# One-column sums of a modulation vector: four blocks in one slot and one bank, or a block a slot and a bank each

## The chip, the cores and the metric

The kernel runs on one core of a Trainium2 chip. The metric is the device time of one execution in microseconds (us), as the median of several runs. TensorE (PE) does the matrix products, VectorE (DVE) and ScalarE (ACT) the work on vectors, GpSimd (POOL) some subtractions, and SyncE (SP) issues most of the transfers. PE's results land in PSUM, which has eight banks; DVE and ACT take them out of there.

## The reference, cut to what matters

An encoder layer is applied to two requests (256 and 1024 rows of 1024 columns). A conditioning vector `c` of each request sets shifts, scales and gates:

```
mod = einsum('bd,de->be', silu(c), ada_w) + ada_b       # e has 6 * 1024 columns
sh1, sc1, gt1, sh2, sc2, gt2 = split(mod, 6)
h = rmsnorm(x, norm1_g) * (1 + sc1) + sh1
z = h @ w_in                                            # latents, q/k/v of two attentions, two gates
...
x = x + gt1 * (merged @ w_out)
h2 = rmsnorm(x, norm2_g) * (1 + sc2) + sh2
...                                                     # feed-forward with gt2
```

`sh1` and `sc1` are needed at once. The other four (gt1, sh2, sc2, gt2) are needed only behind both attentions: this is "the later modulation". `mod` has one value for each column and request.

## The kernel before, in words

Everything runs once through, as a list of stages written out by hand. Products are in float32 split into a rounded high part and a low rest (three products for one), so PE is the busiest engine. The framework that places the instructions on the engines follows the order of the Python text, but lets an instruction that it thinks ready go ahead of one that it thinks is not; buffers of one tag are handed round.

The stage of this change is the windowed (dilated) attention, lines 841 to 961. Its outer loop takes six steps (three head groups by two pairs, line 855), its inner loop ten row blocks `i` (line 935). In a row block PE computes scores (L890, into the banks S0 and S1), DVE adds the bias and finds the extreme (L895), ACT takes the exponential (L900), PE transposes (L910), DVE or ACT copies out (L914, L916), and PE multiplies by the values (L925), which DVE or ACT copies out (L931, L929).

Between these steps the loop draws on generators, that is, on Python functions that issue a few instructions and then `yield`:

- `side` (`filler`, line 672) issues the products of the gates from `block` (line 656; L99). A chunk of 512 or 256 columns takes one bank of the tag "pp" through 24 matmuls, in four draws, and is then copied out by ACT (L665) or DVE (L663). It is drawn 19 times in ten row blocks.
- `side2` (`norms`, line 695) is drawn once in each row block; six of its draws make sums of the same form in "pp" (L711), and one a transpose.
- `more` loads the queries and keys of the next step (L628, and a subtraction by DVE).
- `side3` (`modulation`, line 759) is the one that the change touches. It is drawn three times in two row blocks: 15 draws a step, 90 in all six.

`modulation` goes over eight chunks `c` of 512 columns of `mod`. For each it loads eight blocks of `ada_w` (L765, 256 KB each, tag "ad") and adds each, times the value of `c`, to an accumulator `acc` of 128 x 512 for either request (tag "mo", one buffer; DVE, L768 for the first block, L770 for the others). After each of the eight blocks it yields. What is left is the sum over the 128 partitions of `acc`: a matmul with 128 columns of `acc` as the weights and one column of ones gives 128 sums in one column. Four blocks of 128 columns by two requests make eight matmuls (L775), all into one bank of "pp"; as float32 each is two instructions on PE, so 16 a chunk. Two additions by DVE (line 777, shown at the helper's line L77 as `t<-pp,t`) take the bank's eight columns, add `ada_b` and write `modT`. Then it yields once more: nine draws a chunk, 72 in all.

The tag "pp" has two buffers (lines 354 and 355), shared by `block`, `norms`, `modulation`, the transposed statistics at each step's end (L953, copied by L955) and `gate_rows` (L189). After the six steps what is left of `side` is run out, then `gain_cols` (L184, which reads `modT`) and `gate_rows` (L189, which reads it too) follow.

Of the kernel before, what the change touches and what calls it, by code (L numbers as in the profile page):

```python
# [12 lines left out]
ALU = mybir.AluOpType  # L13
# [3 lines left out]
P = 128  # L17
# [28 lines left out]
def kernel(  # L46
# [8 lines left out]
    nc = tc.nc  # L55
    count = [0]

    def mk(pool, shape, dt=F32, tag=None, bufs=None):
        count[0] += 1
        kw = {}  # L60
        if bufs is not None:
            kw["bufs"] = bufs
        return pool.tile(shape, dt, name=f"{tag or 't'}_{count[0]}", tag=tag or f"u{count[0]}", **kw)
# [12 lines left out]
    def dve_tt(out, a, b, op):  # L76
        nc.vector.tensor_tensor(out=out, in0=a, in1=b, op=op)  # L77
# [30 lines left out]
    ones = mk(const, [P, P])  # L108
    nc.vector.memset(ones, 1.0)
    vecT = mk(const, [P, V_END])  # L110
    modT = mk(const, [P, 6 * KD, 2])
# [106 lines left out]
    def X():  # L218
        return mk(psX[1], [P, 2, 512], tag="X", bufs=4)
# [107 lines left out]
    abT = mk(hcm[1], [P, 6 * KD])  # L327
# [15 lines left out]
    def bank(tag, bufs=1):  # L343
        return mk(psC[1], [P, 512], tag=tag, bufs=bufs)
# [9 lines left out]
    def pp():  # L354
        return bank("pp", 2)
# [397 lines left out]
    def ad_tile(dt=F32):  # L753
        return mk(cpl, [P, 512], dt, tag="ad", bufs=AD)
# [4 lines left out]
    def modulation():  # L759

        for c in range(4, 12):
            acc = mk(cpl, [P, 2, 512], tag="mo", bufs=1)
            for k in range(KD):
                w = ad_tile()
                nc.sync.dma_start(out=w, in_=ada_w[k * P:(k + 1) * P, 512 * c:512 * c + 512])  # L765
                for r in range(2):
                    if k == 0:
                        nc.vector.tensor_scalar(out=acc[:, r], in0=w, scalar1=cT[:, k, r:r + 1], scalar2=None, op0=ALU.mult)  # L768
                    else:
                        nc.vector.scalar_tensor_tensor(out=acc[:, r], in0=w, scalar=cT[:, k, r:r + 1], in1=acc[:, r], op0=ALU.mult, op1=ALU.add)  # L770
                yield
            ps = pp()[:, 0:8]
            for b in range(4):
                for r in range(2):
                    nc.tensor.matmul(ps[:, 2 * b + r:2 * b + r + 1], lhsT=acc[:, r, P * b:P * b + P], rhs=ones[:, 0:1], start=True, stop=True)  # L775
            for r in range(2):
                dve_tt(modT[:, 4 * c:4 * c + 4, r], ps.rearrange("p (b r) -> p b r", r=2)[:, :, r], abT[:, 4 * c:4 * c + 4], ALU.add)
            yield

    SIDE = 19  # L780

# [66 lines left out]
    rest, LD, SPEED = [], 1, 2  # L848

    side, side2, side3 = filler(), norms(), modulation()  # L850
    values(0)
    run(queries_keys(0, 0, qk[0, 0]))
    for _ in range(8):
        next(side)
    for pair, g in steps:
# [96 lines left out]
        ps = pp()  # L952
# [765 lines left out]
    for j in range(4):  # L1718
        ps = X()
# [341 lines left out]
```

## Time and profile before

| | us |
|---|---|
| median of 3 runs | 2418.75 (2415.92 to 2419.02) |
| the profiled execution, its own time | 2418.45 |
| its span, first to last instruction | 2416.6 |
| around the span | 1.85 |

PE is busy for 97% of the span, DVE for 65%, ACT for 44% and POOL for 40%; the mean granted clock of TensorE is 0.981 of the full one. A granted clock of 1.00 is 2.4 GHz and one of 0.50 is 1.2 GHz. PE counts as busy while a matmul is anywhere in it, so that a busy PE may still run slowly. In the views, "PEld" is the loading of weights, an "x" the number of instructions, and the brackets at the end of a row tell how long the engine had been idle and what released it.

### The profile page before, as it was taken

The numbers are of one execution on the slowest core, as the hardware profiler recorded it, in microseconds if no ns is written. First come the engines' busy times: TensorE is split into PE (matmuls) and PEld (weight loads), VectorE is DVE, ScalarE is ACT, GpSimd is POOL, SyncE is SP. The second block draws the span as 40 slices with busy tenths as digits, with TensorE's granted clock in tenths as the row PEclk, the third lists the DMA queues.
The fourth block names the chain that finished last, engine by engine and source line by source line (L and its number), as shares of the span: only waits on it lengthen the run. The fifth ranks groups of instructions, "written<-read, shape, count | busy, mean of one in ns | idle before, by whom it ended". The sixth has DMA issues, their size and how long they took to land. (4 is left out here: it accounts for less than half of the span.)

```text
span 2416.6 us, 36977 instructions
## 1 busy us (share of the span) xinstructions
PE 2332.1 (97%) x13083; PEld 2002.8 (83%) x13083; DVE 1577.8 (65%) x2683; ACT 1074.3 (44%) x2094; POOL 977.4 (40%) x721
## 2 busy tenths in 40 slices
PE   7999999999999999999998989989999999999998
PEld 3889998777787777777776778789999999988786
DVE  4743334788648688888896533476655565567688
ACT  4421212554425477777776433353322232244434
POOL 1023331110135166666677441004565546538330
PEclk9999999999999999999998999999999999999999
DMA  7232225668459833333332753432232222267564
GB/s 267 73 120 88 101 88 176 191 211 260 141 158 303 279 82 83 84 84 87 91 107 75 213 183 118 140 114 88 88 112 83 82 82 103 83 223 246 192 205 164
DMA packets 208019, 342.48 MB, mean 142 GB/s; under 512 B 24365, under 2 KB 86686, under 8 KB 207834
## 3 DMA queue, kind: packets, MB, share of 16 engines
q1 hardware_dynamic: 182238, 311.00, 40.3%
q10 hardware_dynamic: 25596, 29.12, 3.5%
q8 instruction: 103, 1.69, 0.3%
q14 instruction: 82, 0.67, 0.1%
HBM read 236.67 MB, written 94.19 MB: 137 GB/s over the span
## 5 line engine op out<-in xcount | busy, mean ns | idle before, releaser
L243 PE MATMUL X<-t,wh 128*128 128x320 f32 x2864 | 538.4, 310 | 7.0 <-ACT ut L1777 6.8
L243 PEld LDWEIGHTS X<-t,wh 128*128 128x128 f32 x2864 | 451.3, 189 | 7.6 <-ACT ut L1777 7.1
L80 POOL TENSOR_TENSOR pl<-p,ph 128x512 fp32r<-128x512 f32 x224 | 297.3, 1337 | 137.4 <-ACT ph L1190 102.1
L243 PE MATMUL X<-t,wl 128*128 128x320 f32 x1432 | 327.4, 310 | 1.8 <-POOL wl L80 1.0
L243 PEld LDWEIGHTS X<-t,wl 128*128 128x128 f32 x1432 | 240.0, 189 | 2.5 <-POOL wl L80 1.2
L1189 ACT ACTIVATE p<-S 128x512 f32<-128x512 f32 x272 | 163.3, 600 | 106.3 <-issue 40.0
L1171 DVE TENSOR_REDUCE m<-mi 128x1 f32<-128x512 f32 x256 | 173.9, 685 | 35.7 <-PE mi L1170 32.8
L229 ACT CAST wh<-wr 128x512 fp32r<-128x512 f32 x113 | 70.2, 621 | 283.5 <-PE X L243 179.0
L99 PE MATMUL pp<-t,wh 128*128 128x512 f32 (+1 forms) x624 | 190.0, 386 | 1.7 <-DVE sm L955 0.8
L77 DVE TENSOR_TENSOR ut<-X,ut 128x640 f32<-128x640 f32 x126 | 101.4, 818 | 131.2 <-PE X L243 78.7
L1190 ACT ACTIVATE ph<-S 128x512 fp32r<-128x512 f32 x272 | 162.3, 597 | 1.0 <-issue 0.3
L80 POOL TENSOR_TENSOR wl<-R,wh 128x512 fp32r<-128x512 f32 x60 | 98.7, 1646 | 146.1 <-ACT wh L229 146.1
L1871 PE MATMUL Y<-bh,ah 128*128 128x512 f32 x385 | 150.7, 392 | 3.5 <-ACT t L1889 1.9
L1871 PE MATMUL Y<-bh,al 128*128 128x512 f32 x385 | 150.5, 391 | 0.0
L1871 PE MATMUL Y<-bl,ah 128*128 128x512 f32 x385 | 150.4, 391 | 0.0
L77 DVE TENSOR_TENSOR wl<-wr,wh 128x512 fp32r<-128x512 f32 x128 | 117.1, 916 | 45.2 <-ACT wh L229 42.2
L243 PE MATMUL X<-R,wh 128*128 128x320 f32 x736 | 138.1, 309 | 0.0
L77 DVE TENSOR_TENSOR pt<-X,pt 128x640 f32<-128x640 f32 x60 | 48.5, 823 | 134.7 <-PE X L243 83.6
L80 POOL TENSOR_TENSOR wl<-wr,wh 128x512 fp32r<-128x512 f32 (+2 forms) x39 | 46.5, 1194 | 218.6 <-ACT wh L208 104.7
L99 PEld LDWEIGHTS pp<-t,wh 128*128 128x128 f32 x624 | 109.7, 196 | 23.9 <-issue 4.5
L77 DVE TENSOR_TENSOR al<-ar,ah 128x640 fp32r<-128x640 f32 x75 | 79.5, 1060 | 59.6 <-ACT ah L1844 57.0
L77 DVE TENSOR_TENSOR ac<-ac,p 128x512 f32<-128x512 f32 x160 | 110.9, 693 | 9.7 <-ACT p L1189 7.6
(434 smaller groups left out, 5691.8 us busy)
## 6 DMA issues: line engine op xcount, KB each, us to landing
ac_d<-ut SPq DMA_DIRECT2D x77, 320.0 KB
ar<-ac_d SPq DMA_DIRECT2D x75, 320.0 KB
R<-in_w_up_dram SPq DMA_DIRECT2D x84, 256.0 KB
br<-in_w_down_dram SPq DMA_DIRECT2D x77, 256.0 KB
ad<-in_ada_w_dram SPq DMA_DIRECT2D x64, 256.0 KB
rw<-in_w_in_dram SPq DMA_DIRECT2D x20, 512.0 KB
V<-v_d SPq DMA_DIRECT2D x16, 640.0 KB
v<-in_ada_w_dram SPq DMA_DIRECT2D x32, 256.0 KB
```

The costliest lines, as they stand in the source:

```text
L77: nc.vector.tensor_tensor(out=out, in0=a, in1=b, op=op)
L80: nc.gpsimd.tensor_tensor(out=out, in0=a, in1=b, op=op)
L99: nc.tensor.matmul(ps, lhsT=w[k], rhs=x[k], start=(k == 0 and w is wh and x is xh), stop=(k == n - 1 and w is wl))
L229: nc.scalar.copy(out=h, in_=a)
L243: nc.tensor.matmul(ps[:, z, 0:320], lhsT=a[:, k, :], rhs=b[q][k][:, 320 * z:320 * z + 320], start=(j == 0 and i == 0), stop=(j == n - 1 an ...
L1171: nc.vector.reduce_max(out=m2[:, i, c:c + 1], in_=ps, axis=AX.X)
L1189: nc.scalar.activation(out=p_, in_=ps, func=AF.Exp, scale=MSCALE)
L1190: nc.scalar.activation(out=ph, in_=ps, func=AF.Exp, scale=MSCALE)
L1871: nc.tensor.matmul(ps, lhsT=a[:, P * j:P * j + P], rhs=b, start=(f == 0 and a is ah and b is bh), stop=(f == HF - 1 and a is al))
```

## The change

The eight matmuls of a chunk no longer fill one bank in one draw. Each block of 128 columns gets a bank of "pp" of its own, with two matmuls (two requests), and one addition by DVE of 128 x 2 right behind, in which the bias is read with a stride of zero. After the first three blocks the generator yields; after the fourth it does not, so that the first block of the next chunk's `ada_w` is loaded and multiplied in the same draw. A chunk takes eleven draws instead of nine; the last addition falls into draw 89 instead of 72, of the 90 that there are.

```
-            ps = pp()[:, 0:8]
             for b in range(4):
+                ps = pp()[:, 0:2]
                 for r in range(2):
-                    nc.tensor.matmul(ps[:, 2 * b + r:2 * b + r + 1], lhsT=acc[:, r, P * b:P * b + P], rhs=ones[:, 0:1], start=True, stop=True)
-            for r in range(2):
-                dve_tt(modT[:, 4 * c:4 * c + 4, r], ps.rearrange("p (b r) -> p b r", r=2)[:, :, r], abT[:, 4 * c:4 * c + 4], ALU.add)
-            yield
+                    nc.tensor.matmul(ps[:, r:r + 1], lhsT=acc[:, r, P * b:P * b + P], rhs=ones[:, 0:1], start=True, stop=True)
+                f = 4 * c + b
+                dve_tt(modT[:, f, :], ps, abT[:, f:f + 1].broadcast_to([P, 2]), ALU.add)
+                if b < 3:
+                    yield
```

## Rows read from the trace of the kernel before

**Rows 1.** The page: busy time by engine, and the granted clock in 40 slices.

```profile
PE 2332.1 (97%) x13083; PEld 2002.8 (83%) x13083; DVE 1577.8 (65%) x2683; ACT 1074.3 (44%) x2094; POOL 977.4 (40%) x721
...
PEclk9999999999999999999998999999999999999999
```

**Rows 2.** Stretches: us, busy PE, PEld, DVE, ACT, POOL, clock, DMA share, GB/s.

```profile
412.00:636.00 224.00, 218.70 (x1440) 164.50 (x1438) 180.49 (x468) 118.30 (x323) 23.22 (x18) 0.94 0.70 220
636.00:680.00 44.00, 43.19 (x233) 29.94 (x232) 20.76 (x90) 17.24 (x65) 12.17 (x9) 0.93 0.40 109
680.00:727.00 47.00, 46.01 (x251) 39.17 (x248) 27.14 (x38) 11.00 (x20) 12.49 (x7) 1.00 0.54 156
```

**Rows 3.** The instructions of L775, and who waited for them (us, times).

```profile
L775 PE MATMUL pp<-t,mo x128: 164/250/353, 441.5 to 635.0; 128*128 128x1 f32 x128
...
  DVE t L77: 15.0, 8
```

**Rows 4.** Stretches of L775 alone: us, busy PE and PEld, clock, DMA share, GB/s.

```profile
470.00:473.00 3.00, 1.90 (x16) 2.10 (x16) 1.00 0.80 254
...
552.00:556.00 4.00, 2.00 (x16) 2.01 (x16) 1.00 0.84 258
...
sum 30.00, PE 15.79 PEld 16.06; mean PE 1.97 PEld 2.01
```

**Rows 5.** PE in order of time, around the third chunk's sums.

```profile
498.48 0.50 PE L99 MATMUL pp<-t,wl 128*128 128x512 f32 x1
498.82 1.84 PE L775 MATMUL pp<-t,mo 128*128 128x1 f32 x16
500.59 0.62 PE L890 MATMUL S<-R,R 64*128 64x256 f32 x6
```

**Rows 6.** Stretches (columns as in rows 2): an ordinary one, and those at half clock.

```profile
437.00:440.40 3.40, 3.40 (x27) 2.41 (x25) 2.18 (x7) 1.43 (x6) 1.28 (x1) 1.00 0.52 164
447.20:450.60 3.40, 3.40 (x20) 2.77 (x19) 1.69 (x7) 0.78 (x3) 0.72 (x1) 0.50 0.75 228
...
501.80:505.20 3.40, 3.40 (x12) 2.71 (x11) 3.40 (x9) 1.68 (x5) 0.00 (x0) 0.50 0.69 214
...
529.10:532.50 3.40, 3.40 (x12) 2.73 (x11) 3.40 (x9) 2.05 (x6) 0.00 (x0) 0.50 0.62 195
...
583.70:587.10 3.40, 3.40 (x11) 2.71 (x11) 3.40 (x9) 1.09 (x4) 0.00 (x0) 0.50 0.82 276
...
611.00:614.40 3.40, 3.40 (x12) 1.76 (x12) 2.06 (x7) 1.85 (x8) 0.00 (x0) 0.50 0.80 247
...
634.90:641.70 6.80, 6.80 (x24) 5.04 (x24) 4.58 (x17) 2.44 (x10) 3.51 (x4) 0.50 0.13 36
```

**Rows 7.** DVE in order of time, behind the third chunk's sums.

```profile
500.69 0.23 DVE L77 TENSOR_TENSOR t<-pp,t 128x4 f32<-128x4 f32 x2 [3.11 <-PE pp L775]
```

**Rows 8.** Waits of PE, 394 to 727 us: us in total, times, longest.

```profile
PE pp L99 <- DVE sm L955: 0.8, 1, 0.8
...
PE pp L99 <- DVE sm L663: 0.5, 1, 0.5
...
PE pp L99 <- DVE t L77: 0.2, 1, 0.2
```

**Rows 9.** Other users of the two "pp" banks, in the answer on tile pp.

```profile
L711 PE MATMUL pp<-t,sm x40: 164/250/353, 426.1 to 511.2; 128*128 128x1 f32 x40
...
L77 DVE TENSOR_TENSOR t<-pp,t x16: 150/157/164, 443.9 to 635.5; 128x4 f32<-128x4 f32 x16
```

**Rows 10.** The accumulator's instructions on DVE, in the answer on tile mo.

```profile
L770 DVE SCALAR_TENSOR_TENSOR mo<-ad,t,mo x112: 617/743/1785, 413.1 to 632.1; 128x512 f32<-128x512 f32 x112
L768 DVE TENSOR_SCALAR mo<-ad,t x16: 476/480/488, 412.3 to 610.8; 128x512 f32<-128x512 f32 x16
```

**Rows 11.** The first reader of the finished modulation on PE.

```profile
L189 PE MATMUL pp<-t,t x2: 270/274/277, 726.0 to 726.6; 128*16 128x128 f32 x2
```

## The prediction, made before the changed kernel was run

> **What bounds the kernel now.** I read the page first: PE is busy for 97% of the span, no other engine for more than 65%, and the granted clock is below full in some slices [rows 1]. So time can be won only where PE is slowed down or waits. The change lies in the windowed attention, so I then asked for stretches of that stage. From 412 to 636 us, where the later modulation runs, PE is busy for 218.7 of 224 us at a mean clock of 0.94, DVE for 180.5 (43.5 idle); from 636 to 680, the last of the six steps, DVE has 23.2 of 44 us idle; from 680 to 727 the rest of the gates' products runs alone [rows 2]. That last part matters: whatever PE saves before 680 us is handed on, since what follows is a queue of products that starts earlier.
>
> Third, the one-column sums themselves. They are 128 instructions on PE, and DVE's additions wait 15.0 us for them in eight waits, 1.9 each [rows 3]. By stretches, a chunk's sixteen take some 1.97 us of PE, 15.8 for all eight [rows 4], and in order of time they stand in one piece, 16 in 1.84 us between a product and the scores [rows 5]. (In some chunks two go ahead and fourteen follow.)
>
> Last, the clock, by stretches around the sums. An ordinary 3.4 us has clock 1.00. Behind the third chunk's sums (498.8 to 500.6) the clock is 0.50 from 501.8 to 505.2, with PE busy throughout. The same follows in six of the eight chunks: at 447.2, 501.8, 529.1, 583.7 and 611.0 for 3.4 us each, at 634.9 for 6.8 [rows 6]: 23.8 us at 1.2 instead of 2.4 GHz. The second and the fifth chunk, whose sums are as dense [rows 4], show none; at 447.2 the norms' sums came in between too. So the dense sums make a fall of the clock likely, not certain, and no idle PE is needed for it.
>
> **The change, part by part.**
>
> *The clock.* With a block a draw, four PE instructions stand together instead of up to sixteen, about a quarter of 1.97, that is 0.5 us, and a draw comes every 3 us (72 draws from 412 to 635.5). Between them stand products and scores, as in the ordinary stretch. I take it that all six falls go. What that is worth is bounded above by half of 23.8, 11.9 us, if PE alone sets the pace there, and below by nothing, if DVE does. The rows lie in between: at 501.8, 529.1 and 583.7 DVE is busy for all of the 3.4 us, so there a faster PE may only meet a DVE that is behind; at 447.2, 611.0 and 634.9 (13.6 us together) DVE is busy for 1.69, 2.06 and 4.58 us and has time to spare [rows 6]. I count these three in full, 6.8 us. Of the other three (5.1) I count a third, 1.7: DVE is behind there partly because it had stood for the sums itself, 3.11 us before 500.7 [rows 7], and that wait shrinks. **-8.5 us.**
>
> *The sums on PE.* As many instructions of the same form, so 15.8 us as before [rows 4]: 0. A bound for a worse case is one break of the pipeline for each of 24 more groups.
>
> *The additions on DVE.* Sixteen at 0.157 us [rows 9] become 32 of half the size; at the same price each, 2.5 us more on DVE, beside 43.5 us idle [rows 2]: 0 on the path. Uncovered it would cost those 2.5.
>
> *DVE's waits.* Each addition stands in DVE's queue behind the accumulator's work and waits for PE, and the next scores' L895 stands behind it; behind the third chunk that held DVE for 3.11 us [rows 7]. A quarter of the sums is a quarter of the wait, so 32 times 0.47 is again 15 us: 0. If a wait stays at 1.9, 24 more are 45 us, as much as all of DVE's idle time; then L895 is late next, and behind it ACT's exponential and PE's transposes.
>
> *The banks.* 24 more tenants go through the two "pp" banks, of which a chunk of the gates' products holds one nearly always. If the other is still waiting for its addition when the next chunk starts, PE stands before L99. The trace shows this price: 0.8 us once behind the statistics' copy, 0.5 behind a chunk's copy, 0.2 behind the addition itself [rows 8], 1.5 us together for 21 tenants other than the gates (8 chunks of sums, 6 of the norms' and one transpose [rows 9], 6 statistics). By that rate 24 more cost 1.7; the ends are 0 and 24 x 0.8 = 19 us. I take the rate, since the additions are short. **+1.7 us.** ACT's and DVE's copies of the chunks (L665, L663) keep their place.
>
> *What moves.* The modulation ends with draw 89 instead of 72. Ten of its 64 blocks thereby move into the last step, each with a 256 KB load on SP's queue and two instructions of DVE at 0.74 us (0.48 for a first block) [rows 10], some 14 us of DVE. From 636 to 680 DVE has 23.2 us idle, and the DMA share is 0.40 against 0.70 before [rows 2], so both fit, and up to 636 us DVE has that much less to do. If they do not fit, the last step gives back up to 2 us. The first reader on PE stands at 726 us [rows 11], 45 behind the new end: 0. The next chunk's first block (L768) now follows the fourth addition in one draw; it must wait for those sums before it overwrites "mo", as it had to before.
>
> *A rule to weigh.* The falls of the clock follow the sums, and eight handovers of a bank make six falls [rows 4, 6]; the trace does not tell density from handover. The Trainium skill, "TensorE: Matmul & The Clock Gate", section "A second HAM failure mode: psum-queue depth-cycling", says that a PE which goes round the banks every iteration idles for moments between groups of matmuls, and that this makes the clock swing. By that rule more banks would mean more falls, against the density that I hold responsible; that sentence holds nothing that the sum rests on. The gates' products, which change banks every 24 matmuls, run from 680 to 727 at 1.00 [rows 2].
>
> *The sum.* -8.5 + 1.7 = -6.8 us. The profiled execution took 2418.45, so 2411.65 on its scale; the median of the three runs is 0.3 above it, hence **2412.0 us** as a median.
>
> **The rivals.**
>
> 1. *No difference that counts.* The falls go, but DVE fills the place (it is at its full 3.4 us in three of six), or the framework puts two or three blocks' sums together again, since it orders by what it thinks ready, and the falls stay. That would be the change that doesn't do what it says. For it: DVE at 81% of 412 to 636. Against: DVE is idle in three stretches, and the accumulator's work is thinned out by two draws in eleven. Time: a gain of 0 to 2 with the banks' 1.7 against it, about 2419.5.
> 2. *The banks turn it round.* PE stands at the first matmul of a gates' chunk because the second bank waits for an addition that DVE has not come to. Price 0.8 us [rows 8]; from 11 such stalls of 24 on it eats the 8.5, from 17 on the kernel is slower by over 0.2%. With 18: -8.5 + 14.4, about 2424.6. For it: DVE was up to 3.1 us out of step with PE at such an addition [rows 7]. Against: only three stalls in 21 tenants so far.
> 3. *Handovers make the falls.* If each of the 32 handovers drew falls as the eight did (six of eight), there would be 24; at 1.4 us each (8.5 for six) that is 34 us in place of 8.5, with the banks' 1.7 about 2446. Against: the run of gates at 1.00. It is this that the rule of the Trainium skill's page named above would mean here.
>
> **How the numbers follow.** About 0.2% (4.8 us) is what a measurement of this kernel can tell from no change. The forecast case (falls gone, PE gains) has 0.62: its own range is -12 to -3, 2407 to 2416, and about three quarters of it, 0.46, lie beyond 4.8 us. Rival 1 has 0.22, rival 2 has 0.12, rival 3 has 0.04. Faster 0.46, same 0.16 + 0.22 + 0.01 of rival 2 = 0.39, slower 0.15. The range leaves out rival 3 and the worse half of rival 2: low is 2418.75 - 11.9 less a little for DVE's shorter waits, 2405; high is 2424, where some 17 stalls have eaten the gain.
>
> **What would show it.** Right: L775 in pieces of two and four; clock 1.00 behind each group of sums; L189 some 7 us earlier than 726; 15 us or so of DVE waits in 32 pieces; few waits of "PE pp L99 <- DVE t L77". Wrong: falls of the clock still behind the sums, or clock 1.00 with L189 still at 726 (DVE's pace), or many waits before L99.

## The result: slower, and where the time went

| | before | after |
|---|---|---|
| median, runs side by side (us) | 2417.34 (2412.36 to 2419.02, 4 runs) | 2437.31 (2428.57 to 2440.80, 4 runs) |
| ratio, 95% interval | 1 | 1.0079 (1.0058 to 1.0100) |
| the profiled execution: own time, span, clock | 2418.45, 2416.6, 0.981 | 2437.3, 2435.5, 0.977 |

The changed kernel is 0.8% slower, where 0.3% faster was forecast. In the changed kernel lines behind the edit stand one higher (L890 is now L891, L895 L896, L925 L926, L955 L956); L775 and L77 are the same.

**What came as foretold.** The sums now stand on PE in pieces of two or four, and behind the first three chunks' the clock no longer falls. The first view is PE in order of time around a block of the third chunk, whose sixteen stood together before [rows 5]; the second a stretch of 103 us from the end of the first step into the third (columns as in [rows 2]), in which 48 of the sums' instructions lie and, before, three of the six falls of [rows 6] did.

```profile
506.58 0.62 PE L891 MATMUL S<-R,R 64*128 64x256 f32 x6
507.13 0.61 PE L775 MATMUL pp<-t,mo 128*128 128x1 f32 x4
```

```profile
437.00:540.00 103.00, 102.18 (x730) 77.80 (x728) 82.94 (x214) 57.70 (x155) 15.63 (x11) 1.00 0.60 194
```

**Where the time went.** I cut both profiles at the first scores and at each step's transpose of the statistics (L953, now L954). First the kernel before: all six steps, the fifth, the sixth.

```profile
414.30:680.30 266.00, 261.81 (x1671) 194.61 (x1672) 199.22 (x554) 134.91 (x387) 35.39 (x27) 0.94 0.65 200
599.60:644.20 44.60, 43.97 (x251) 32.07 (x250) 32.53 (x100) 21.68 (x65) 7.95 (x7) 0.89 0.57 180
644.20:680.30 36.10, 35.28 (x203) 24.33 (x202) 16.39 (x76) 14.92 (x57) 8.74 (x6) 1.00 0.45 122
```

Then the same three stretches of the changed kernel, and its two longest at half clock in the sixth and fifth step.

```profile
412.80:698.80 286.00, 272.64 (x1672) 200.02 (x1672) 204.73 (x572) 135.08 (x387) 35.52 (x27) 0.90 0.59 187
601.10:651.50 50.40, 45.23 (x245) 32.66 (x243) 37.29 (x105) 21.54 (x65) 7.43 (x7) 0.88 0.55 174
651.50:698.80 47.30, 44.68 (x226) 31.41 (x224) 28.44 (x102) 15.35 (x57) 8.64 (x6) 0.84 0.42 116
...
643.10:653.30 10.20, 8.53 (x27) 5.91 (x29) 6.51 (x21) 2.03 (x7) 2.74 (x3) 0.50 0.27 85
656.80:670.50 13.70, 13.70 (x46) 8.76 (x45) 5.73 (x20) 3.69 (x15) 0.00 (x0) 0.50 0.37 117
```

PE has as many instructions (1671 and 1672), yet the six steps are 20.0 us longer, 17.0 of it in the fifth and sixth (97.7 against 80.7). Stretch less busy time is PE's idle time: 4.2 us before, 13.4 after, 9.2 more. The stretches at half clock add up to 30.7 us before and 54.6 after; 24 us at half of the clock are 12 us of work. 9.2 and 12 are 21, all of the 20. Of the 24, 10.3 lie in the first step, where the changed kernel is at half clock for 20.5 us from 414.4, before any of the sums; in the fifth and sixth step it is 27.3 us against 10.2. In the sixth step DVE is busy for 28.4 us in place of 16.4. The first reader of the finished modulation (L189) starts at 743.8 in place of 726.0 [rows 11], so that nearly all of the 18.9 us by which the span grew are lost before it.

**What PE waits for.** The three longest of six lines in the answer on PE's waits in the fifth and sixth step (us, times, longest). All six come to 7.7 us in nine waits; before, it was 1.3 us in three.

```profile
PE pp L99 <- DVE wl L77: 4.8, 2, 3.7
PE pp L775 <- DVE sm L956: 1.3, 1, 1.3
PE pp L775 <- DVE mo L770: 0.6, 2, 0.3
```

None of these three is a product that waits until a sum's bank is read. All are waits for late work of DVE: the low parts of a gate's weights, the statistics' copy (whose bank the sums want), the accumulator. And DVE had stood for the sums: in all 25.1 us in 16 waits, where it was 15.0 in 8 [rows 3], and in these two steps 11.7 us in 7 against 1.8 in 2. The first row is of the whole answer on L775, the others DVE in order of time around one addition.

```profile
  DVE t L77: 25.1, 16
```

```profile
664.01 0.16 DVE L77 TENSOR_TENSOR t<-pp,t 128x2 f32<-128x2 f32 x1 [2.92 <-PE pp L775]
664.09 0.87 DVE L768 TENSOR_SCALAR mo<-ad,t 128x512 f32<-128x512 f32 x2
664.88 0.28 DVE L896 CUSTOM_DVE_ANT_0 sm<-S,bs 128x128 f32<-128x128 f32 x1
```

An addition of 0.16 us kept DVE for 2.92, and the next scores' extreme (L896) came behind it and the next chunk's first block. PE was at half clock then (656.8 to 670.5), with three of the gates' products and four with the values ahead of the block's sums. Three of the 16 waits, 9.0 of the 25.1 us, end in or just behind a stretch at half clock (at 555.8, 650.5 and 664.0): the slow clock lengthens the waits too, so their total is not purely a cause.

The longest stand (a stretch in which PE waits) has a second cause on top. First POOL, then DVE, then PE, each in order of time:

```profile
640.49 1.26 POOL L80 TENSOR_TENSOR qk<-qk,qk 32x512 f32<-32x512 f32 x1 [7.05 <-DVE qk L683]
641.72 1.25 POOL L80 TENSOR_TENSOR wl<-wr,wh 128x512 fp32r<-128x512 f32 x1
```

```profile
640.48 3.04 DVE L770 SCALAR_TENSOR_TENSOR mo<-ad,t,mo 128x512 f32<-128x512 f32 x1
...
644.05 0.67 DVE L77 TENSOR_TENSOR wl<-wr,wh 128x512 fp32r<-128x512 f32 x1
```

```profile
644.77 0.79 PE L99 MATMUL pp<-t,wl 128*128 128x512 f32 x1 [3.73 <-DVE wl L77]
```

A block of the accumulator that otherwise takes 0.74 us [rows 10] takes 3.04, longer than the two POOL instructions that run back to back beside it (1.26 and 1.25), and the split weights that PE wants stand behind it. The Trainium skill, "SBUF — State Buffer", section "Who interferes with whom", says that a DVE instruction with two inputs in SBUF contends with a GpSimd instruction that reads SBUF. These rows agree: 0.74, 1.26 and 1.25 are 3.25, and it is DVE that was held up, although its row starts 0.01 us ahead of POOL's. Before, the longest block took 1.785 [rows 10].

### The profile page after: what moved, and what is told of

Same layout as the page of the kernel before. It is cut to its first block, busy times and chain, and to the rows that moved or that the text cites. A ratio compares the mean times of both kernels' runs of the same rounds, so it can differ in the third digit from the quotient of the medians.

```text
span 2435.5 us, 36969 instructions
## 1 busy us (share of the span) xinstructions
PE 2342.8 (96%) x13083; PEld 2008.7 (82%) x13083; DVE 1576.5 (65%) x2699; ACT 1074.8 (44%) x2094; POOL 970.3 (40%) x721
## 5 line engine op out<-in xcount | busy, mean ns | idle before, releaser
L77 DVE TENSOR_TENSOR ut<-X,ut 128x640 f32<-128x640 f32 x126 | 101.5, 819 | 131.2 <-PE X L243 78.7
L80 POOL TENSOR_TENSOR wl<-R,wh 128x512 fp32r<-128x512 f32 x60 | 93.3, 1556 | 146.0 <-ACT wh L229 146.0
L77 DVE TENSOR_TENSOR wl<-wr,wh 128x512 fp32r<-128x512 f32 x128 | 110.9, 868 | 44.8 <-ACT wh L229 41.3
L77 DVE TENSOR_TENSOR pt<-X,pt 128x640 f32<-128x640 f32 x60 | 48.6, 823 | 134.6 <-PE X L243 83.6
L99 PE MATMUL pp<-t,wl 128*128 128x512 f32 (+1 forms) x312 | 117.5, 377 | 4.8 <-DVE wl L77 4.8
L77 DVE TENSOR_TENSOR al<-ar,ah 128x640 fp32r<-128x640 f32 x75 | 78.0, 1039 | 64.0 <-ACT ah L1845 61.2
```

Source lines behind the costliest of these rows:

```text
L80: nc.gpsimd.tensor_tensor(out=out, in0=a, in1=b, op=op)
L99: nc.tensor.matmul(ps, lhsT=w[k], rhs=x[k], start=(k == 0 and w is wh and x is xh), stop=(k == n - 1 and w is wl))
```

## The experiments

Each kernel was run beside the kernel before; ratios are to those runs, whose medians were 2417.8 to 2420.2. Executions of one kernel scatter by 7 to 20 us, and a profile is one of them, so verdicts rest on ratios, and profiles say only what stands where.

### First: is it the late end, the banks, or the small pieces?

**e1**: the changed kernel, drawn 19 times a step.

```
-                if part == 0 or i % 2:
+                if part == 0 or i < NT - 1:
```

> The changed kernel, but the modulation is drawn 19 times a step instead of 15, so that its 89 draws end two thirds through the fifth step, a little before the place where the old kernel ended; blocks, banks and additions as in the changed kernel. Theory P (place: the loss comes from the work that moved into the last step, from 651 to 699 us in the changed kernel, where 11 us were lost, and from the end of the fifth, where 6 were): the loss goes, and with the dense sums gone too it is at or below the kernel before, 2408 to 2418. Theory B (banks: the 24 more tenants of the two pp banks cost the time): no better than the changed kernel, 2432 to 2442, since the tenants come closer together.

2432.94, ratio 1.0064 (1.0042 to 1.0086). The last step was 42.1 us, but the first two took 109.1, where before they had 94.3; 40.9 us of them were at half clock, where before it was 13.6. Whether the quicker draws made that is not shown. So a loss of 0.6% is there with an early end too, but in a kernel with a change of its own.

**e2**: the kernel before, with two empty draws behind each chunk: dense sums, ending as late as the changed kernel.

```
-            yield
+            for _ in range(3 if c < 11 else 1):
+                yield
```

> The kernel before, with its sums in one bank and one draw, but two empty draws behind each chunk, so that the accumulation ends with draw 85 as in the changed kernel. Theory P: slow like the changed kernel, 2430 to 2445, with falls of the clock behind the sums besides. Theory B: like the kernel before, 2413 to 2421, since no bank is handed over more often.

2425.95, 1.0031 (1.0016 to 1.0046). A late end alone costs 0.3%, less than half of the loss.

**e3**: the changed kernel, each block's sums in the free eighth bank.

```
-                ps = pp()[:, 0:2]
+                ps = bank("one")[:, 0:2]
```

> The changed kernel, with its sums in a bank of their own, the eighth of PSUM, which nothing else uses in this stage, in place of the two shared pp banks. Theory P: still slow, 2430 to 2440. Theory B: the loss goes, 2408 to 2420.

2430.56, 1.0045 (1.0022 to 1.0067). Less than the change's 1.0079, but the two intervals overlap; by the two ratios more than half of the loss is there without any handover of the sums in "pp".

**e4**: the changed kernel, two blocks in a draw, nine draws a chunk: 32 banks and 32 additions still.

```
-                if b < 3:
+                if b == 1:
                     yield
```

> The changed kernel, but it yields only after the second block: two blocks with their four matmuls in one draw, two in the next, so that the modulation ends with draw 73 instead of 89 (72 before), at its old place. Still 32 tenants of the pp banks. Theory P: no loss, and fewer falls of the clock than before: 2409 to 2418. Theory B: slow, 2430 to 2440, since the tenants are as many.

2420.33, 1.0008 (0.9988 to 1.0029). **e5** goes further: no yield between the blocks at all.

> The changed kernel with no yield after the first three blocks: four banks and four additions a chunk, all in one draw, nine draws a chunk, so the modulation ends with draw 72 as before. Banks alone, without the spreading. If the banks are what costs (theory banks), PE stands four times in a row for a bank in each chunk and the time stays near the changed kernel's, 2430 or more. If the later end and what then meets at the passage from the fifth to the sixth step costs (theory passage), the last step has its 36 us again and the time is that of the kernel before within 5 us, 2414 to 2424.

2421.61, 1.0011 (0.9999 to 1.0023). So neither the 24 more banks nor the 24 more additions cost anything that counts as long as they come together and early.

### Second: is it the particular stands between the fifth and sixth step?

In several profiles PE stood there for the statistics' copy (L956), which waits in DVE's queue behind the rotation of the keys, or for the weights beside two of POOL's instructions. **e6** takes the statistics out of "pp"; **e7** also does the rotation's product on DVE; **e8** does both to the kernel before.

```
-        ps = pp()
+        ps = bank("one")
         nc.tensor.transpose(ps[0:40, 0:P], stat, ident)
...
-        pool_tt(sw, sw, si, ALU.mult)
+        (dve_tt if x.shape[0] == 32 else pool_tt)(sw, sw, si, ALU.mult)
```

> The changed kernel, with the transposed statistics at each step's end in the eighth bank, which is free, in place of one of the two pp banks. Theory passage, by the statistics: the sums and the gates no longer wait at about 653 us for the copy of the statistics, which stands in DVE's queue behind the rotation of the keys; the long stretch at half clock behind it goes, the last step falls from 47 to 40 us or less, and the time to some 2427 to 2431. Theory passage, by the weights: the stand of 3 to 4 us at 640 us, before a gates' product whose split weights are late, is untouched, and so is the time, 2434 to 2440. Theory place: nothing changes, since the modulation still lies in the last step.

2436.82, 1.0076 (1.0059 to 1.0093).

> As the kernel with the statistics in the eighth bank, and besides the multiplication of the keys' rotation is done by DVE and not by POOL, so that POOL has the split of the weights alone at about 641 us and DVE's chain behind the rotation has no handover to POOL in it. Theory passage: both stands go, no half clock of more than 7 us between 640 and 665, the last step at 36 to 40 us, the time that of the kernel before or below, 2410 to 2422. Theory place (ten blocks in the last step cost by themselves): the last step stays at 44 or more and the time at 2428 or more.

2434.98, 1.0068 (1.0048 to 1.0088).

> The kernel before with the same two edits, statistics in the eighth bank and the rotation's multiplication on DVE. Theory passage: the kernel before has only a stand of about 1 us there, so it gains little, 0 to 4 us: 2414 to 2420. If it gains 10 or more, the two edits are worth something everywhere, and what they give the changed kernel says nothing of the change.

2416.21, 0.9982 (0.9966 to 0.9998). The two longest lines of PE's waits in the last two steps of e7:

```profile
PE S L891 <- DVE stat L896: 1.9, 2, 1.7
PE pp L99 <- DVE wl L77: 1.2, 1, 1.2
```

The wait for the statistics is gone and that for the weights is 1.2 in place of 4.8, but another of 1.7 stands in their place, now for the scores, and behind it, from 651.1, the clock is at half for 13.7 us. My theory that these two stands made the loss is thereby refuted: with both gone or shortened the loss stays. It seems that DVE is late, and that what PE misses first is a matter of the moment. What e8 gives the kernel before is small, but outside its interval.

### Third: spread against late, and DVE against PE in the last chunk

**e9**: the changed kernel with nine draws a chunk, by loading four of the eight blocks in pairs (`if k not in (0, 2): yield`). **e10**: two by two, with two empty draws behind each chunk.

> The changed kernel, sums block by block as there, but the loads of a chunk in six draws in place of eight (the first and second block together, and the third and fourth), so that a chunk takes nine draws and the last addition falls into draw 73 in place of 89. Theory late (ten blocks of the modulation in the last step are what costs): the last step is at 36 to 38 us, the time 2415 to 2424. Theory spread (sums spread over four draws are what costs, wherever they lie): 2428 to 2438. If both have a part, in between.

2436.02, 1.0084 (1.0059 to 1.0108). The last step was 36.7 us, but the fifth 55.3. It is no clean undoing of the late end, though: the sums now wait for the paired accumulation, as PE's waits in its six steps show (its lines are shifted by one).

```profile
PE pp L776 <- DVE mo L770: 5.4, 6, 2.3
```

> The sums in two draws of two blocks, as in the kernel that yields after the second block only, with two empty draws behind each chunk, so that the modulation ends as late as in the changed kernel. Theory late: 2426 to 2438, as the kernel with the dense sums and empty draws (1.0031) or worse. Theory spread: as the two-by-two kernel, 2417 to 2424.

2429.85, 1.0052 (1.0033 to 1.0071). The two-by-two form, free when it ends early (e4), costs 0.5% when it ends late.

**e11** leaves DVE's accumulation out of the last chunk (`elif c < 11`), **e12** its one-column sums.

> The changed kernel, in which the last chunk's blocks are loaded but only the first is multiplied into the accumulator: 14 instructions of DVE at 0.74 us are left out, nearly all of them in the last step, nothing on PE or SP. If DVE's accumulation in the last step is what holds PE up and lets its clock fall, the last step falls from 47 to 40 us or less and the time to 2424 to 2430. If it is the sums or the loads, it stays at 2434 to 2440.

2429.40, 1.0050 (1.0032 to 1.0067).

> The changed kernel, in which the last chunk's sixteen one-column instructions on PE and their four banks are left out, while DVE's accumulation and four additions (of the bias to itself) stay. If the sums in the last step cost by themselves, by breaking up PE's work and the turn of the banks, the time falls by more than their own 2 us, to 2425 to 2431. If DVE's accumulation is the cause, by 2 us or less, 2433 to 2439.

2431.03, 1.0052 (1.0032 to 1.0072). Either takes some 0.3% off, at the edge of what the interval tells from the change itself, and neither brings the kernel before back: these two don't tell the causes apart.

### Fourth: is it DVE's queue, or the scattered sums on PE?

**e13**: ACT does each block's addition.

```
-                dve_tt(modT[:, f, :], ps, abT[:, f:f + 1].broadcast_to([P, 2]), ALU.add)
+                nc.scalar.activation(out=modT[:, f, :], in_=ps, func=AF.Identity, scale=1.0, bias=abT[:, f:f + 1])
```

> The changed kernel, with each block's addition done by ACT (an activation with the bias) in place of DVE, so that DVE never waits for the one-column sums. Theory DVE's queue: the 18 to 30 us that DVE waits for L775 are gone, PE's stands behind late work of DVE fall from some 9 us more than before to 4 or less, and the time falls to 2415 to 2426. Theory PE (scattered sums cost there): it stays at 2430 to 2438.

2448.40, 1.0115 (1.0093 to 1.0138), worse, against both theories as I had put them. The wait went with the addition to ACT, but DVE did not get free of it: the next chunk's first block (L768) overwrites the accumulator and waits for the same sums. The waits of ACT and of DVE for the sums in the six steps, and PE's longest:

```profile
ACT t L777 <- PE pp L775: 30.6, 22, 4.6
```

```profile
DVE mo L768 <- PE pp L775: 12.2, 5, 4.7
```

```profile
PE pp L775 <- DVE mo L770: 9.8, 2, 9.6
```

The stand of 9.6 us lies at the very end, where one of the last blocks of the accumulator comes behind 4.42 us of DVE's work for the stage's end. So e13 adds waits on ACT without freeing DVE, and it does not decide between the two theories.

**e14**: sums block by block in four draws, ending as late, but in one bank (the eighth), with the two additions once, behind the fourth block.

```
+            ps = bank("one")[:, 0:8]
             for b in range(4):
-                ps = pp()[:, 0:2]
...
                 if b < 3:
                     yield
+            for r in range(2):
+                dve_tt(modT[:, 4 * c:4 * c + 4, r], ps.rearrange("p (b r) -> p b r", r=2)[:, :, r], abT[:, 4 * c:4 * c + 4], ALU.add)
```

> The changed kernel, sums still block by block in four draws and as late as there, but all four blocks into one bank, the free eighth, and the two additions by DVE once, behind the fourth block, as in the kernel before. The spreading on PE alone. Theory DVE's queue: eight waits of DVE in place of 32, 2415 to 2428 (a late end cost 0.3% with dense sums). Theory PE: 2430 to 2438.

2422.46, 1.0014 (1.0000 to 1.0029). The scattered sums on PE and the late end are all still there, and by the two ratios about four fifths of the loss are gone; so these two alone do not make it. What e14 takes away is the additions by block together with the sums' place in "pp". e3, which takes away only the second, is at 1.0045, halfway, and its interval overlaps both others a little: the two are not told apart. DVE's waits for the sums in the six steps, and the stretch of those:

```profile
DVE t L77 <- PE one L775: 8.7, 5, 5.4
```

```profile
413.20:680.20 267.00, 258.42 (x1655) 191.38 (x1656) 199.80 (x553) 135.31 (x387) 35.22 (x27) 0.94 0.64 198
```

Five waits in place of 16, and 267.0 us in place of 286.0. A last group of sums, 16 instructions, falls behind the stretch, and with it the waits are 10.7 us in 6. The 267.0 flatters e14: its profiled execution took 2417.73, one of the fastest of the twelve.

**e15** is the control for e13: the kernel before with a chunk's additions on ACT.

> The kernel before with the additions of a chunk on ACT, four activations of one block each in place of DVE's two. Theory DVE's queue: DVE's 15 us of waits for the dense sums go, of which little lies on the path, 2411 to 2420. If ACT, which then waits for the sums in its own queue, comes late to the exponentials, 2420 to 2430.

2424.24, 1.0018 (1.0006 to 1.0031): with dense sums ACT's waits are 10.8 us in 6 and DVE's, in L768, 12.1 in 4, and they cost little.

### Fifth: can the one bank beat both?

**e16** is e14 with e9's six draws of loads; **e17** is e14 with `if b == 1` (two by two, early); **e18** is e17 with the rotation's product on DVE.

> One bank of its own for a chunk, sums block by block in four draws, two additions at the end, and the loads in six draws in place of eight, so that the last addition falls into draw 73. If the late end is the rest of the cost, the last step is at 36 to 38 us again and the first five keep their gain: 2406 to 2416. If the paired loads hold DVE up, or the gain of the five steps was chance, 2416 to 2426.

2425.72, 1.0032 (1.0015 to 1.0049), no gain from the earlier end, which I put down to the paired loads. Beside e9 it tells more: both have the paired loads, four draws and an early end, and they differ as e14 and the change do, in bank and additions. Here too the joined form is faster (1.0032 against 1.0084), and the intervals are apart.

> The same bank and additions, sums in two draws of two blocks, loads in eight draws as in the kernel before; the last addition in draw 73. No paired loads, so nothing new on DVE: 2408 to 2416 if the one bank of its own and the halved group of sums are worth what the clock showed, 2416 to 2424 if not.

2417.90, 1.0004 (0.9987 to 1.0021).

> As the two-by-two kernel in one bank, and the multiplication of the keys' rotation on DVE in place of POOL. The kernel before gained 4 us from this with the statistics in the eighth bank; if the rotation was the better half of that, 2 to 4 us below the kernel without it, 2405 to 2414; else the same as it.

2415.10, 0.9995 (0.9979 to 1.0010). Neither can be told from the kernel before. The one version below both kernels is e8, and it owes nothing to the change.

### The runs side by side

The two right columns are from the profiles: the waits of the additions' engine, DVE (e13: ACT), for the sums in the six steps, and PE's idle time there (stretch less busy).

| kernel | sums | additions | ends | ratio | waits for sums | PE idle |
|---|---|---|---|---|---|---|
| before | one draw | joined | early | 1 | 15.0 in 8 | 4.2 |
| e5 | one draw | 4 apiece | early | 1.0011 | 17.1 in 23 | 6.6 |
| e17 | two draws, own bank | joined | early | 1.0004 | 11.7 in 8 | 7.7 |
| e4 | two draws | by block | early | 1.0008 | 15.3 in 22 | 6.5 |
| e16 | four draws, own bank | joined | early, paired loads | 1.0032 | 5.5 in 5 | 10.6 |
| e1 | four draws | by block | early, quick draws | 1.0064 | 18.3 in 14 | 11.9 |
| e9 | four draws | by block | early, paired loads | 1.0084 | 18.3 in 15 | 14.6 |
| e2 | one draw | joined | late | 1.0031 | 9.8 in 7 | 10.9 |
| e14 | four draws, own bank | joined | late | 1.0014 | 8.7 in 5 | 8.6 |
| e10 | two draws | by block | late | 1.0052 | 23.0 in 26 | 10.6 |
| e3 | four draws, own bank | by block | late | 1.0045 | 22.9 in 16 | 16.7 |
| after | four draws | by block | late | 1.0079 | 25.1 in 16 | 13.4 |
| e13 | four draws | by block, ACT | late | 1.0115 | 30.6 in 22 | 25.0 |

With the sums in four draws, reading each block by itself costs, with a late end (the change against e14) and with an early one (e9 against e16). Each pair also moves the sums out of "pp", so what is shown is the cost of by-block additions and shared banks together. With one or two draws and an early end neither costs anything (e5, e4, e17); a late end adds 0.3 to 0.4% there (e2, e10).

PE's idle time is what goes with the ratio. The eight kernels within 0.2% of the kernel before (itself, e4, e5, e8, e14, e15, e17, e18) have 3.2 to 8.6 us of it in the six steps, the twelve others, from 1.0031 on, 10.6 to 25.0. Time at half clock does not part them (30.7 to 54.6 us against 41.0 to 78.5), nor do the waits for sums by their total: e5 has 17.1 us at 1.0011, e2 9.8 at 1.0031. That the waits, by holding DVE's queue, are what makes PE idle in the spread kernels is read from the rows of the change; no run tried it by itself.

## Why the prediction was wrong, point by point

**The step that failed is "DVE's waits"**, and with it "What moves"; the clock's term, below, went the other way by more microseconds. "DVE's waits" said that a quarter of the sums is a quarter of the wait, so 32 times 0.47 and 15 us as before: 0. The wait was not in proportion to the sums: 16 of the 32 additions waited, 1.57 us each, nearly as long as the 1.88 before. DVE waits until PE, in its own order, comes to them, behind whatever products stand ahead; a single block's addition waited 2.92 us at 664, at half clock. The total went from 15.0 to 25.1. The other half of that step, "if a wait stays at 1.9, 24 more are 45 us; then L895 is late next", named the right mechanism with an upper end that was not reached, and I gave it no price on PE and no chance of its own. PE's idle time, which the sum has nowhere but in the banks' 1.7, rose by 9.2 us. With the additions joined and the sums in a bank of their own, e14 has 10.7 us of waits, 4.4 us more of idle time than the kernel before, and 1.0014. How much of that is the waits and how much the banks stays open.

**What moves: 0, up to +2.** The prediction let ten blocks move into the last step; by the trace it was eight, 16 instructions of 10.8 us. They fit into DVE's idle time by their sum (28.4 us busy in 47.3), as I had said, but not by their place: the sixth step is 11.2 us longer. With dense sums the same move costs 0.3% (e2), some 7 us. It is not needed for the loss, though: e1 and e9 end early and lose 0.6 and 0.8%, with changes of their own. I had covered a sum of busy times with a sum of idle times; what counts is what stands behind a late instruction.

**The clock: -8.5.** In this profile this term missed by the most: 12 us lost in place of 8.5 won. The falls behind the first three chunks' sums went, as foretold. But others came (the next at 547.5, in the fourth chunk's, behind a stand of 0.7), 54.6 us at half clock against 30.7, and the long ones lie in the fifth and sixth step: 643.1 begins within the stand of 3.73 that ends at 644.77, 656.8 some two microseconds behind one of 1.3 for the statistics' copy. In e2, e3 and e7 too a stretch of 10.2 to 20.5 us begins during or a few microseconds behind a stand of 1.7 to 4.4 us there. But such a stretch does not make a kernel slow: e17 has one of 13.7 us from 647.6, begun within a stand of 2.4, at 1.0004, and e14 one of 17.1 from 634.3, behind a stand of 2.2, at 1.0014. That a stand brings the fall is what the rows suggest; it was not tried by itself, and [rows 6] show falls without any stand. Part of the difference is chance: the first step has 10.2 us at half clock in the profile of before and 20.5 here, but 23.9 to 27.3 in e4, e5 and e8, at 1.0008, 1.0011 and 0.9982. As to the gain, no run has it: e17, with half the group and no late end, is at 1.0004, and its clock is at half for 47.8 us in the six steps. So that spreading the sums frees PE of half clock is not borne out, nor what it would be worth.

**The sums on PE, 0, the additions, 0, the banks, +1.7.** The instructions and their durations stand as before (250 ns; an addition 159), and e5, which has all 32 banks and additions in one draw, is at 1.0011: right to within its interval. There PE stands 2.7 us, in five waits, until an addition has read its bank, where before it was 0.2; that is near the 1.7 forecast. The own bank of e3 may take 0.3% off the change, so where additions are late, banks may cost up to that; the intervals leave it open.

**The rivals.** Rival 2, that PE stands before the gates' products, came nearest, at 2424.6; but its stands were to be for the sums' additions, 0.8 us each, and the ones that came were for split weights and statistics that DVE was late with, up to 3.7, with the clock behind them, which I had not priced. Rival 3 asked for falls at every handover: in the 103 us from 437 with three chunks' twelve handovers there was none, and e5 has as many handovers as the change without its loss. The rule of the Trainium skill ("TensorE: Matmul & The Clock Gate", section "A second HAM failure mode: psum-queue depth-cycling"), that short idle moments of PE between groups make the clock swing, fits the last two steps, where PE idles around the long falls (1.3 us before 654.9); that going round the banks is what makes them, these runs don't bear out.

**What stays open**: how the loss is shared between late end, by-block additions and banks. They don't add up (e2, e10, e3 and the change itself); by-block additions in four draws with a bank of their own and an early end were not tried, nor joined ones in "pp"; and spread additions with an early end were tried only with quicker draws or paired loads (e1, e9), which brought losses of their own.

## What to carry to other kernels

Price a small instruction that waits for another engine by its wait, not by its duration, and by what stands behind it in its engine's queue; cutting a group of products into four can hand the engine that reads them more waits of nearly the old length (16 of 1.57 us for 8 of 1.88), not quarters of one. If PE's work is to be spread, let it collect in one bank and read it once, at the end: this was almost free here (1.0014), and the same reads one by one were not (1.0045 in a bank of their own, 1.0079 in the shared ones). And when a generator's draws get more, look at what its end now meets: idle time in sum is no cover for an instruction that is late.

## What the runs showed of the hardware that I had not expected

A block of DVE (128 x 512, 0.74 us) took 3.04 us beside two instructions of POOL in a row, and in e6 2.97; in e7, where the rotation's product is no longer one of the two, the longest is 1.82. The kernel's time did not follow (1.0076 and 1.0068).

In several profiles a short stand of PE between the fifth and sixth step goes with 10 to 20 us at half clock, while the falls behind dense sums last 3.4 to 6.8 [rows 6]. At half clock PE is busy throughout 656.8 to 670.5, with 46 products in 13.7 us; an ordinary stretch has 27 in 3.4 [rows 6].
